# First query and key products together while x arrives, first value products around the row norm, and program order on three engines until then

## The chip, the cores and the metric

The kernel runs on one core of a Trainium2 chip. The metric is device time in microseconds (us) for one launch. Five engines work side by side: TensorE (PE, with its weight loads as PEld), VectorE (DVE), ScalarE (ACT), GpSimd (POOL) and SyncE (SP), which issues all transfers between memory and the chip. Each engine takes its instructions in one fixed order and waits at an instruction until what it needs is there.

## The reference

One inference step of an encoder layer over 576 new rows plus 16 learned rows (592 in all, `T`), width 2048. The part that matters here is the beginning:

```
h = x * rsqrt(mean(x*x) + eps) * g                # RMSNorm of every row
z = h @ w_in                                      # 2048 -> 3904 columns
q, k, v of 8 differential heads = slices of z     # 128 columns each
... two softmaxes per head with a shared relative-position bias, their difference times v
... a second group of latent-attention heads, output projection, SwiGLU feed-forward, final norm
```

`q`, `k` and `v` of head 0 are the first three 128-column slices that the kernel makes. The norm's factor of a row is a scalar, so it can be applied after the product.

## The kernel before, in words

Every float32 product is split: each operand becomes a high and a low part (`xh`, `xl`; `wh`, `wl`), and three products are added up in PSUM (`mm3`, three matmuls for each of two halves of 296 rows; called a triple below). ScalarE casts the high part, VectorE subtracts to get the low part. So every chunk of x and every block of weights passes ScalarE and then VectorE before TensorE can use it.

The stage in question opens the program. x arrives in four column groups of 512 columns (`load_x`), each in six row tiles (`tok`) with seven transfers. For each of 16 chunks of 128 columns, `transpose_x` lets TensorE transpose the six tiles into PSUM (`pxt`, one two-bank tile, for even chunks; `pxa` and `pxb`, single banks, for odd ones), ScalarE and VectorE split the result with the gain into `xh`, `xl`, VectorE copies the plain transpose to `xt`, and SyncE stores `xt` to `xspill` for the residual addition much later. `xt` has three buffers (`Z_BUFS`), so the copy of a chunk waits until the store of three chunks before has landed. After chunk 3 of each group the squares of the group's six tiles are summed on ScalarE (`ssp`).

Between the transposes stand the triples of head 0's queries alone (`first = project(ps0, ...)`), one per chunk. Then come the norm (`ss`, `rc`, `rb`; six small matmuls into `prb` spread the factor over all partitions), the bias table (`ptr`, `trs`, `trow`, and `tsk`, eight broadcast stores of 328 KB), and then `projections()`: keys and values of head 0, then queries, keys and values of heads 1 to 7. `natural` transposes keys and values back for the outputs, and `diff_attend` does the attention of a head; its first matmuls write `sp`. Weights come in blocks of 1024 x 128 (`wr`, 512 KB), two per projection.

TensorE's order is the order in which the code calls it. For the projections and the attention that order is set by `Streams`, a planner in the kernel: it keeps a clock `now` that each matmul moves on, banks (`sp`, `tp`, `po`) with times at which they come free, and streams with ranks; the projections are the filler of lowest rank. VectorE's, ScalarE's and SyncE's orders are chosen when the program is built, by a scheduler that takes what it thinks ready first. GpSimd has a few memsets in this stage.

Of the kernel before, what the change touches and what calls it, by code (L numbers as in the profile page):

```python
# [111 lines left out]
        self.tc.keep_in_program_order(self.pe.transpose(out, in_, identity))  # L112


@with_exitstack
def encoder_step(
    ctx: ExitStack,
# [16 lines left out]
    S.preload_act_table_set("natural_log_exp_and_others")  # L134

    def load(dst, src):
        nc.sync.dma_start(dst, src)

    def store(dst, src):
        nc.sync.dma_start(dst, src)  # L140

    def const(name, shape, src):
        t = cp.tile(shape, F32, name=name)
# [19 lines left out]
    def rsqrt(r, v):  # L163

        S.activation(r, v, AF.Ln)
        S.activation(r, r, AF.Exp, scale=-0.5)
        V.tensor_tensor(v, v, r, op=ALU.mult)
        V.scalar_tensor_tensor(v, v, -0.5, r, op0=ALU.mult, op1=ALU.mult)
        V.scalar_tensor_tensor(r, v, 1.5, r, op0=ALU.add, op1=ALU.mult)
# [144 lines left out]
    with ExitStack() as ph:  # L314
# [7 lines left out]
        def pjt():  # L322
            return pj.tile([P, 2, 512], F32, name="ps", tag="ps")
# [4 lines left out]
        def tbank(name="tp"):  # L328
            return pst.tile([P, 512], F32, name=name, tag="tp")
# [11 lines left out]


        tok = [(0, OWN), (OWN, P), (208, 88), (TH, P), (424, P), (552, 40)]
        ps0 = pjt()
        with tc.tile_pool(name="xn", bufs=1) as xn:
            ssp = az.tile([P, 6, 4], F32, name="ssp")
            V.memset(ssp, 1.0)
            junk = xn.tile([P, 512], F32, name="junk")
            xt_in = {}

            def load_x(cg):
                cs = slice(cg * 512, (cg + 1) * 512)
                for j, (o, n) in enumerate(tok):
                    t = xn.tile([P, 512], F32, name="xn", tag=f"xn{j}", bufs=2)
                    if j == 0:
                        load(t[0:NS, :], x_sample[:, cs])
                        load(t[NS:OWN, :], meta[:, cs])
                    else:
                        load(t[0:n, :], x_prompt[o - OWN:o - OWN + n, cs])
                    xt_in[cg, j] = t  # L360

            def transpose_x(kc):
                cg, k = kc // 4, kc % 4
                if kc % 2 == 0:
                    sp = sbig("pxt")
                    banks = [sp[:, 0, 0:TH], sp[:, 1, 0:TH]]
                else:
                    banks = [tbank("pxa")[:, 0:TH], pso.tile([P, 512], F32, name="pxb", tag="po")[:, 0:TH]]
                for j, (o, n) in enumerate(tok):
                    b = o // TH  # L370
                    PE.transpose(banks[b][:, o - b * TH:o - b * TH + n],
                                 xt_in[cg, j][0:n, k * P:(k + 1) * P], ident[0:n, 0:n])
                xt = ztile("xt")
                g = gA[:, kc:kc + 1]
                if kc % 2 == 0:
                    split_scaled(hv(xh[kc]), hv(xl[kc]), ev(sp), g)
                    V.tensor_copy(hv(xt), ev(sp))
                else:
                    for b in range(2):
                        c = slice(b * TH, (b + 1) * TH)  # L380
                        split_scaled(xh[kc][:, c], xl[kc][:, c], banks[b], g)
                        V.tensor_copy(xt[:, c], banks[b])
                for o, n, c in KEPT:
                    store(xspill[kc, :, c:c + n], xt[:, o:o + n])
                if k == 3:
                    for j, (o, n) in enumerate(tok):
                        S.activation(junk[0:n], xt_in[cg, j][0:n], AF.Square, accum_out=ssp[0:n, j, cg:cg + 1])
                    if cg + 2 < 4:
                        load_x(cg + 2)

            load_x(0)
            gains = xn.tile([P, P], F32, name="gains")
            V.memset(gains, 0.0)
            rows = 0
            for g in (g_attn, g_ffn, g_fin, g_q, g_kv, g_sub):
                n = g.shape[0] // P
                load(gains[rows:rows + n, :], g.rearrange("(c p) -> c p", p=P))
                rows += n
# [6 lines left out]
            first = project(ps0, w_in[:, 0:P], xs1)  # L405
# [18 lines left out]
        ss = az.tile([P, 6], F32, name="ss")  # L424
        rc = az.tile([P, 6], F32, name="rc")
        V.reduce_sum(ss, ssp, axis=AX.X)
        V.tensor_scalar(ss, ss, 1.0 / D, EPS, op0=ALU.mult, op1=ALU.add)
        rsqrt(rc, ss)
        pb = sbig("prb")
        for j, (o, n) in enumerate(tok):  # L430
            b = o // TH
            PE.matmul(pb[:, b, o - b * TH:o - b * TH + n], rc[0:n, j:j + 1].to_broadcast([n, P]),
                      ident[0:n, 0:n], start=True, stop=True)
        V.tensor_copy(hv(rb), ev(pb))

        with tc.tile_pool(name="xc", bufs=1, side="right") as xc:

            oh = xc.tile([32, NREL], F32, name="oh")
            load(oh, c_onehot)
            rbt = xc.tile([32, H], F32, name="rbt")  # L440
            load(rbt, rel_bias)
            ptr = sbig("ptr")
            trs = xc.tile([H, NREL], F32, name="trs")
            for i, (a, b) in enumerate(((0, 512), (512, NREL))):
                PE.matmul(ptr[0:H, i, 0:b - a], rbt, oh[:, a:b], start=True, stop=True)
                V.tensor_copy(trs[:, a:b], ptr[0:H, i, 0:b - a])
            store(trow, trs)
            for h in range(H):
                nc.sync.dma_start(tsk[h], trow[h:h + 1, :].to_broadcast([P, NREL]))

            lamt = xc.tile([P, 4, DH], F32, name="lamt")
            load(lamt, lam_p.rearrange("a b -> (a b)").unsqueeze(0).to_broadcast([P, 4 * DH]).rearrange(
                "p (a b) -> p a b", a=4))
            lprod = xc.tile([P, 2, DH], F32, name="lprod")
            lsum = xc.tile([P, 2], F32, name="lsum")
            V.tensor_tensor(lprod, lamt[:, 0:4:2, :], lamt[:, 1:4:2, :], op=ALU.mult)
            V.reduce_sum(lsum, lprod, axis=AX.X)
            S.activation(lsum, lsum, AF.Exp)
            V.memset(lamv[:, 0:1], 1.0)
            V.tensor_tensor(lamv[:, 1:2], lsum[:, 0:1], lsum[:, 1:2], op=ALU.subtract)  # L460
            V.tensor_scalar(lamv[:, 1:2], lamv[:, 1:2], LAM_INIT, None, op0=ALU.add)
            V.tensor_scalar(g08, g08, 1.0 - LAM_INIT, None, op0=ALU.mult)

        zl_cm = tc.tile_pool(name="zl", bufs=1, side="right")
        zl = zl_cm.__enter__()
# [110 lines left out]

        def projections():
            for h in range(H):
                ps = ps0 if h == 0 else pjt()
# [10 lines left out]
                ps = pjt()  # L590
                yield from project(ps, w_in[:, OFF_K + h * P:OFF_K + (h + 1) * P], xs1)
                if h >= 1:
                    yield [nat[2 * h - 1], nat[2 * h - 2]]
                z = ztile()
# [3 lines left out]
                split(kh[:, 0:T], kl[:, 0:T], z)  # L598
                nat[2 * h] = st.spawn(0, keys(h, z, kh, kl))

                ps = pjt()
                yield from project(ps, w_in[:, OFF_V + h * P:OFF_V + (h + 1) * P], xs1)
                if h >= 2:
                    yield [att[h - 2]]
                z = ztile()
                V.tensor_tensor(hv(z), ev(ps), hv(rb), op=ALU.mult)
                vh = ap.tile([P, 6, P], F32R, name="vh", bufs=2)
                vl = ap.tile([P, 6, P], F32R, name="vl", bufs=2)
                nat[2 * h + 1] = st.spawn(0, values(h, z, vh, vl))
# [10 lines left out]
        for name in ("sp", "tp", "po"):  # L620
            st.bank(name, 1)
        st.spawn(9, projections())
        st.run()

# [816 lines left out]
```

## Time and profile before

| what | value |
|---|---|
| median of 3 runs | 2577.13 us (2576.43 to 2582.49) |
| the profiled execution's own time | 2573.65 us |
| its span, first to last instruction | 2571.8 us |
| mean granted TensorE clock | 0.985 |
| TensorE busy | 2458.2 us, 96% |
| VectorE busy | 1839.6 us, 72% |
| ScalarE busy | 1056.4 us, 41% |
| transfers | 307.74 MB, mean 120 GB/s |

The profiled execution is 3.5 us below the median of the runs. Times inside the trace are counted from the span's start. A timeline row reads: start, duration, engine, line, operation, output<-inputs, shape, count, and in brackets the idle time before it with what ended it. A waits row reads: who waited for whom, us in total, times, longest.

### The profile page before, as it was taken

The numbers are of one execution on the slowest core, as the hardware profiler recorded it, in microseconds if no ns is written. First come the engines' busy times: TensorE is split into PE (matmuls) and PEld (weight loads), VectorE is DVE, ScalarE is ACT, GpSimd is POOL, SyncE is SP. The second block draws the span as 40 slices with busy tenths as digits, with TensorE's granted clock in tenths as the row PEclk, the third lists the DMA queues.
The fourth block names the chain that finished last, engine by engine and source line by source line (L and its number), as shares of the span: only waits on it lengthen the run. The fifth ranks groups of instructions, "written<-read, shape, count | busy, mean of one in ns | idle before, by whom it ended". The sixth has DMA issues, their size and how long they took to land. (4 is left out here: it accounts for less than half of the span.)

```text
span 2571.8 us, 44874 instructions
## 1 busy us (share of the span) xinstructions
PE 2458.2 (96%) x17847; PEld 2394.0 (93%) x17847; DVE 1839.6 (72%) x2955; ACT 1056.4 (41%) x1879; POOL 770.6 (30%) x614
## 2 busy tenths in 40 slices
PE   6999999989999999999999999999999899999997
PEld 5999999988999888999999999999999799999997
DVE  5455555556555568877777777777778999999975
ACT  5234333334443444333333333333334444444445
POOL 0000000000000164554645546454553322222236
PEclk9999999999999899999999999999999899999999
DMA  6433222334332453333333333333344643452334
GB/s 205 132 89 87 79 81 82 85 99 131 93 94 76 154 155 108 122 131 117 122 102 118 131 117 129 108 110 127 117 135 141 212 151 95 147 163 83 109 100 148
DMA packets 330564, 307.74 MB, mean 120 GB/s; under 512 B 24707, under 2 KB 298506, under 8 KB 330354
## 3 DMA queue, kind: packets, MB, share of 16 engines
q1 hardware_dynamic: 330354, 304.87, 37.5%
q8 instruction: 140, 2.29, 0.4%
q14 instruction: 70, 0.57, 0.1%
HBM read 250.82 MB, written 56.68 MB: 120 GB/s over the span
## 5 line engine op out<-in xcount | busy, mean ns | idle before, releaser
L1051 PE MATMUL m<-bh,wh 128*128 128x288 f32 x3584 | 969.1, 296 | 12.5 <-ACT wh L156 10.4
L1051 PE MATMUL m<-bl,wh 128*128 128x288 f32 x3584 | 967.7, 295 | 0.0
L1051 PEld LDWEIGHTS m<-bh,wh 128*128 128x128 f32 x3584 | 674.2, 188 | 15.1 <-ACT wh L156 12.7
L1051 PEld LDWEIGHTS m<-bl,wh 128*128 128x128 f32 x3584 | 677.9, 189 | 0.1
L1055 PE MATMUL m<-bh,wl 128*128 128x288 f32 x3584 | 588.7, 299 | 29.5 <-DVE wl L153 27.0
L1020 POOL TENSOR_TENSOR ws<-raw 128x512 f32<-128x512 f32 x256 | 364.7, 1433 | 753.4 <-DVE wl L153 517.7
L1055 PEld LDWEIGHTS m<-bh,wl 128*128 128x128 f32 x3584 | 511.8, 189 | 47.0 <-DVE wl L153 46.0
L156 ACT ACTIVATE wh<-ws 128x512 fp32r<-128x512 f32 (+1 forms) x340 | 288.6, 849 | 471.6 <-PE m L1051 341.4
L153 DVE TENSOR_TENSOR wl<-ws,wh 128x512 fp32r<-128x512 f32 (+1 forms) x340 | 380.5, 1124 | 57.4 <-ACT wh L156 52.8
L153 DVE TENSOR_TENSOR wl<-raw,wh 128x512 fp32r<-128x512 f32 x416 | 401.6, 986 | 13.8 <-ACT wh L156 13.2
L156 ACT ACTIVATE wh<-raw 128x512 fp32r<-128x512 f32 x416 | 248.0, 626 | 334.5 <-PE m L1051 303.5
L108 PE MATMUL ps<-xh,wh 128*128 128x296 f32 x992 | 229.5, 313 | 6.5 <-ACT wh L156 6.5
L108 PE MATMUL ps<-xl,wh 128*128 128x296 f32 x992 | 219.8, 303 | 0.0
L108 PE MATMUL ps<-xh,wl 128*128 128x296 f32 x992 | 219.2, 303 | 0.0
L108 PEld LDWEIGHTS ps<-xh,wh 128*128 128x128 f32 x992 | 163.8, 193 | 10.4 <-ACT wh L156 6.7
L108 PEld LDWEIGHTS ps<-xl,wh 128*128 128x128 f32 x992 | 164.6, 192 | 0.4 <-DVE xl L161 0.2
L108 PEld LDWEIGHTS ps<-xh,wl 128*128 128x128 f32 x992 | 164.2, 192 | 0.3 <-DVE wl L153 0.3
L1020 DVE TENSOR_TENSOR ws<-ws,raw 128x512 f32<-128x512 f32 x128 | 96.1, 755 | 90.4 <-POOL ws L1020 85.4
L153 DVE TENSOR_TENSOR wl<-wr,wh 128x1024 fp32r<-128x1024 f32 (+1 forms) x110 | 117.8, 1071 | 44.4 <-ACT wh L156 42.5
L1272 DVE TENSOR_TENSOR y<-y,m 128x288 f32<-128x288 f32 x280 | 125.6, 449 | 19.3 <-PE m L1055 18.1
L156 ACT ACTIVATE wh<-wr 128x1024 fp32r<-128x1024 f32 (+1 forms) x110 | 101.8, 930 | 79.9 <-PE ps L108 71.4
L518 POOL MEMSET bias<- 64x64 f32 x8 | 1.4, 180 | 413.7 <-DMA bias<-tsk 184.8
(361 smaller groups left out, 3420.0 us busy)
## 6 DMA issues: line engine op xcount, KB each, us to landing
raw<-in_ffn_w_gate SPq DMA_DIRECT2D x44, 1024.0 KB, 7.2
raw<-in_ffn_w_up SPq DMA_DIRECT2D x44, 1024.0 KB, 6.0
raw<-in_ffn_w_down SPq DMA_DIRECT2D x40, 1024.0 KB, 5.4
wr<-in_w_in SPq DMA_DIRECT2D x60, 512.0 KB, 3.7
actspill<-c SPq DMA_DIRECT2D x44, 288.0 KB, 2.2
sumspill<-c SPq DMA_DIRECT2D x20, 576.0 KB, 3.0
bl<-sumspill SPq DMA_DIRECT2D x80, 144.0 KB, 3.1
bl<-actspill SPq DMA_DIRECT2D x68, 144.0 KB, 3.9
```

What stands on the lines that cost most here:

```text
L108: self.tc.keep_in_program_order(self.pe.matmul(out, lhsT, rhs, start=start, stop=stop))
L153: V.tensor_tensor(lo, src, f32(hi), op=ALU.subtract)
L156: S.activation(hi, src, AF.Copy)
L518: G.memset(bias[0:64, 464:528], -BIG)
L1020: engine.tensor_tensor(w[:, k:k + m, :], pick(xs), pick(ys), op=op)
L1051: PE.matmul(banks[p], wh[:, k, :], x, start=first and new and k == 0 and x is hi, stop=False, skip_group_check=not new)
L1055: PE.matmul(banks[p], wl[:, k, :], hi, start=False, stop=last and k == n - 1, skip_group_check=not new)
L1272: V.tensor_tensor(c, c, banks[p], op=ALU.add)
```

## The change

- A small class `Engine` wraps VectorE, ScalarE and SyncE. While its flag is set, the instructions keep the order of the code; the flag is set from the first load of the stage to the end of the bias table's broadcasts.
- The loads of the gains, the one-hot table `oh` and `rel_bias` come ahead of x. The weights of head 0's first half of queries and of keys come after the first x group, those of the second half after the second, and the third and fourth x group follow at once (four buffers a tile in place of two). All of this stands ahead of the first `xspill` store.
- The bias table's two matmuls come ahead of the first transpose.
- Each chunk now has two triples, queries (`psq`) and keys (`psk`). The squares are spread over the chunks of a group.
- The values of head 0 (`psv`, in the bank pair of `sp`) follow: eight triples, the norm's six small matmuls, eight triples. The first value weights are loaded and cast at chunk 10.
- `projections()` starts with all three of head 0 done; the planner's bank `sp` starts taken and comes free when `psv` has been read.

The core of the diff:

```diff
+class Engine:
...
+        def call(*args, **kwargs):
+            ins = issue(*args, **kwargs)
+            return self.tc.keep_in_program_order(ins) if self.ordered else ins
...
-    V, S, G = nc.vector, nc.scalar, nc.gpsimd
+    V, S, Q, G = Engine(tc, nc.vector), Engine(tc, nc.scalar), Engine(tc, nc.sync), nc.gpsimd
...
+        psq, psk, psv = pjt(), pjt(), None
+        for e in (V, S, Q):
+            e.ordered = True
...
-                    t = xn.tile([P, 512], F32, name="xn", tag=f"xn{j}", bufs=2)
+                    t = xn.tile([P, 512], F32, name="xn", tag=f"xn{j}", bufs=4)
...
             load_x(0)
+            raws = [raw_weights(wp, 0, 0), raw_weights(xn, 0, OFF_K)]
             load_x(1)
+            raws += [raw_weights(wp, 8 * P, 0), raw_weights(xn, 8 * P, OFF_K)]
+            load_x(2)
+            load_x(3)
...
             transpose_x(0)
+            ws = [split_raw(wp, raws[0])]
+            transpose_x(1)
+            ws.append(split_raw(xn, raws[1]))
             for kc in range(KC):
-                if kc + 1 < KC:
-                    transpose_x(kc + 1)
-                next(first)
+                if kc:
+                    if kc + 1 < KC:
+                        transpose_x(kc + 1)
+                    squares(kc // 4, ((), (0,), (1, 2), (3, 4, 5))[kc % 4])
+                if kc in (4, 6):
+                    ws.append(split_raw((wp, xn)[kc // 2 - 2], raws[kc // 2]))
+                elif kc == 8:
+                    store(trow, trs)
+                elif kc == 10:
+                    raws.append(raw_weights(wp, 0, OFF_V))
+                    ws.append(split_raw(wp, raws[4]))
+                elif kc == 12:
+                    raws.append(raw_weights(wp, 8 * P, OFF_V))
+                for i, ps in enumerate((psq, psk)):
+                    wh, wl = ws[kc // 8 * 2 + i]
+                    mm3([ps[:, 0, 0:TH], ps[:, 1, 0:TH]], wh[:, kc % 8, :], wl[:, kc % 8, :],
+                        halves(xh[kc]), halves(xl[kc]), kc == 0, kc == KC - 1)
+            psv = sbig("psv")
...
+            rsqrt(rc, ss)
+            first_values(0)
+            ws.append(split_raw(wp, raws[5]))
...
+            first_values(1)
...
+            for h in range(H):
+                Q.dma_start(tsk[h], trow[h:h + 1, :].to_broadcast([P, NREL]))
+        for e in (V, S, Q):
+            e.ordered = False
```

Three places show how the instructions move. First SyncE's queue, where the first stores of `xt` (chunks 0 and 1) stand. Before, they follow the second x group and one block of weights:

```order
L137 DMA xn<-in_x_prompt 40x512
L137 DMA wr<-in_w_in 128x8x128
L140 DMA xspill<-xt 128x64
L140 DMA xspill<-xt 128x512
L140 DMA xspill<-xt 128x64
L140 DMA xspill<-xt 128x512
L137 DMA wr<-in_w_in 128x8x128
```

Now, from the fourth x group on:

```order
L125 DMA xn<-in_x_sample 64x512
L125 DMA xn<-in_meta_tokens 16x512
L125 DMA xn<-in_x_prompt 128x512
L125 DMA xn<-in_x_prompt 88x512
L125 DMA xn<-in_x_prompt 128x512 x2
L125 DMA xn<-in_x_prompt 40x512
L125 DMA lamt<-in_diff_lambda 128x256
L125 DMA xspill<-xt 128x64
L125 DMA xspill<-xt 128x512
```

The first store has moved from behind two x groups and one weight block to behind all four x groups, four weight blocks and `lamt`.

Second, ScalarE around chunks 11 and 12 (`xh_103` and `xh_104`; `wh<-wr` is the cast of a weight block, `junk` a square). Before:

```order
L160 ACTIVATE xh_103<-pxa,gT 128x296
L160 ACTIVATE xh_103<-pxb,gT 128x296
L387 ACTIVATE junk,ssp<-xn 80x512
L387 ACTIVATE junk,ssp<-xn 128x512
L387 ACTIVATE junk,ssp<-xn 88x512
L387 ACTIVATE junk,ssp<-xn 128x512 x2
L387 ACTIVATE junk,ssp<-xn 40x512
L160 ACTIVATE xh_104<-pxt,gT 128x592
```

Now:

```order
L125 ACTIVATE xh_103<-pxa,gT 128x296
L125 ACTIVATE xh_103<-pxb,gT 128x296
L125 ACTIVATE junk,ssp<-xn 128x512
L125 ACTIVATE junk,ssp<-xn 88x512
L125 ACTIVATE wh<-wr 128x1024
L125 ACTIVATE xh_104<-pxt,gT 128x592
```

The cast of the first value weights now stands between the two chunks; the load of those weights is issued on SyncE directly behind the two stores of chunk 11.

Third, TensorE at chunks 0 and 1 (`xh_92`, `xh_93`). Before:

```order
L108 MATMUL ps<-xh_92,wh 128x296 x2
L108 MATMUL ps<-xl_108,wh 128x296 x2
L108 MATMUL ps<-xh_92,wl 128x296 x2
L112 MATMUL pxt<-ident,xn 128x80
L112 MATMUL pxt<-ident,xn 128x128
```

Now:

```order
L108 MATMUL ps<-xh_92,wh 128x296 x2
L108 MATMUL ps<-xl_108,wh 128x296 x2
L108 MATMUL ps<-xh_92,wl 128x296 x2
L108 MATMUL ps<-xh_92,wh 128x296 x2
L108 MATMUL ps<-xl_108,wh 128x296 x2
L108 MATMUL ps<-xh_92,wl 128x296 x2
L112 MATMUL pxt<-ident,xn 128x80
L112 MATMUL pxt<-ident,xn 128x128
```

A second triple, that of the keys, stands between the transposes of two chunks. Further down, 62 triples stand ahead of the first score matmul (`sp`) of head 0 before and 71 now: 48 of head 0 in both, then 14 and 23 of head 1's queries and keys, because the `natural` transposes of head 0's keys no longer stand among its value triples. At the first score of heads 1, 2 and 3 the counts are 125, 181 and 236 before and 132, 187 and 238 now; by the end of head 3 both stand at 256.

More of the change, by code (lines that the diff above doesn't have):

```diff
@@ L112, in transpose, with __init__, __getattr__ @@
         self.tc.keep_in_program_order(self.pe.transpose(out, in_, identity))
+class Engine:
+    def __init__(self, tc, engine):
+        self.tc, self.engine, self.ordered = tc, engine, False
+    def __getattr__(self, name):
+        issue = getattr(self.engine, name)
+        def call(*args, **kwargs):
+            ins = issue(*args, **kwargs)
+            return self.tc.keep_in_program_order(ins) if self.ordered else ins
+        return call
 @with_exitstack
@@ L343, in encoder_step @@
         tok = [(0, OWN), (OWN, P), (208, 88), (TH, P), (424, P), (552, 40)]
-        ps0 = pjt()
-        with tc.tile_pool(name="xn", bufs=1) as xn:
+        psq, psk, psv = pjt(), pjt(), None
+        for e in (V, S, Q):
+            e.ordered = True
+        with tc.tile_pool(name="xn", bufs=1) as xn, tc.tile_pool(name="xc", bufs=1, side="right") as xc:
+            gains = xn.tile([P, P], F32, name="gains")
+            V.memset(gains, 0.0)
+            rows = 0
+            for g in (g_attn, g_ffn, g_fin, g_q, g_kv, g_sub):
+                n = g.shape[0] // P
+                load(gains[rows:rows + n, :], g.rearrange("(c p) -> c p", p=P))
+                rows += n
+            oh = xc.tile([32, NREL], F32, name="oh")
+            load(oh, c_onehot)
+            rbt = xc.tile([32, H], F32, name="rbt")
+            load(rbt, rel_bias)
             ssp = az.tile([P, 6, 4], F32, name="ssp")
@@ L384, in transpose_x, with squares, raw_weights, split_raw @@
                     store(xspill[kc, :, c:c + n], xt[:, o:o + n])
[L385 to L389, printed above, removed]
-            load_x(0)
[L392 to L398, printed above, removed]
-            load_x(1)
+            def squares(cg, js):
+                for j in js:
+                    n = tok[j][1]
+                    S.activation(junk[0:n], xt_in[cg, j][0:n], AF.Square, accum_out=ssp[0:n, j, cg:cg + 1])
+            def raw_weights(pool, r0, c0):
+                wr = pool.tile([P, 8, P], F32, name="wr", tag="wr", bufs=WR_BUFS)
+                load(wr, w_in[r0:r0 + 8 * P, c0:c0 + P].rearrange("(k p) c -> p k c", p=P))
+                return wr
+            def split_raw(pool, wr):
+                wh = pool.tile([P, 8, P], F32R, name="wh", tag="wh", bufs=WH_BUFS)
+                wl = pool.tile([P, 8, P], F32R, name="wl", tag="wl", bufs=WH_BUFS)
+                split(wh, wl, wr)
+                return wh, wl
+            load_x(0)
+            raws = [raw_weights(wp, 0, 0), raw_weights(xn, 0, OFF_K)]
+            load_x(1)
+            raws += [raw_weights(wp, 8 * P, 0), raw_weights(xn, 8 * P, OFF_K)]
+            load_x(2)
+            load_x(3)
+            lamt = xc.tile([P, 4, DH], F32, name="lamt")
+            load(lamt, lam_p.rearrange("a b -> (a b)").unsqueeze(0).to_broadcast([P, 4 * DH]).rearrange(
+                "p (a b) -> p a b", a=4))
             pg = tbank("pg")
@@ L404, in encoder_step @@
             gA, gF, gE, gq, gkv, g08 = (gT[:, a:b] for a, b in ((0, 16), (16, 32), (32, 48), (48, 52), (52, 54), (54, 55)))
-            first = project(ps0, w_in[:, 0:P], xs1)
+            trs = xc.tile([H, NREL], F32, name="trs")
+            ptr = sbig("ptr")
+            for i, (a, b) in enumerate(((0, 512), (512, NREL))):
+                PE.matmul(ptr[0:H, i, 0:b - a], rbt, oh[:, a:b], start=True, stop=True)
+                V.tensor_copy(trs[:, a:b], ptr[0:H, i, 0:b - a])
             transpose_x(0)
+            ws = [split_raw(wp, raws[0])]
@@ new lines, in encoder_step, with first_values @@
+            psv = sbig("psv")
+            def first_values(hf):
+                wh, wl = ws[4 + hf]
+                for k in range(8):
+                    kc = 8 * hf + k
+                    mm3([psv[:, 0, 0:TH], psv[:, 1, 0:TH]], wh[:, k, :], wl[:, k, :],
+                        halves(xh[kc]), halves(xl[kc]), kc == 0, kc == KC - 1)
+            ss = az.tile([P, 6], F32, name="ss")
+            rc = az.tile([P, 6], F32, name="rc")
+            V.reduce_sum(ss, ssp, axis=AX.X)
+            V.tensor_scalar(ss, ss, 1.0 / D, EPS, op0=ALU.mult, op1=ALU.add)
@@ new lines, in encoder_step @@
+            rsqrt(rc, ss)
+            first_values(0)
+            ws.append(split_raw(wp, raws[5]))
+            pb = [tbank("prb"), pso.tile([P, 512], F32, name="prb", tag="po")]
+            for j, (o, n) in enumerate(tok):
+                b = o // TH
+                PE.matmul(pb[b][:, o - b * TH:o - b * TH + n], rc[0:n, j:j + 1].to_broadcast([n, P]),
+                          ident[0:n, 0:n], start=True, stop=True)
+            for b in range(2):
+                V.tensor_copy(rb[:, b * TH:(b + 1) * TH], pb[b][:, 0:TH])
@@ new lines, in encoder_step @@
+            first_values(1)
+            lprod = xc.tile([P, 2, DH], F32, name="lprod")
+            lsum = xc.tile([P, 2], F32, name="lsum")
+            V.tensor_tensor(lprod, lamt[:, 0:4:2, :], lamt[:, 1:4:2, :], op=ALU.mult)
+            V.reduce_sum(lsum, lprod, axis=AX.X)
+            S.activation(lsum, lsum, AF.Exp)
+            V.memset(lamv[:, 0:1], 1.0)
+            V.tensor_tensor(lamv[:, 1:2], lsum[:, 0:1], lsum[:, 1:2], op=ALU.subtract)
+            V.tensor_scalar(lamv[:, 1:2], lamv[:, 1:2], LAM_INIT, None, op0=ALU.add)
@@ L422, in encoder_step @@
             G.memset(pt_b[b][:, 0:NS], 0.0)
[L424 to L462, printed above, removed]
         zl_cm = tc.tile_pool(name="zl", bufs=1, side="right")
@@ L599, in projections @@
                 nat[2 * h] = st.spawn(0, keys(h, z, kh, kl))
-                ps = pjt()
-                yield from project(ps, w_in[:, OFF_V + h * P:OFF_V + (h + 1) * P], xs1)
+                ps = pjt() if h else psv
+                if h:
+                    yield from project(ps, w_in[:, OFF_V + h * P:OFF_V + (h + 1) * P], xs1)
                 if h >= 2:
@@ L606, in projections @@
                 V.tensor_tensor(hv(z), ev(ps), hv(rb), op=ALU.mult)
+                if h == 0:
+                    st.give("sp", 1.5)
                 vh = ap.tile([P, 6, P], F32R, name="vh", bufs=2)
@@ L618, in projections @@
                 V.tensor_tensor(hv(zs[i]), ev(ps), hv(rb), op=ALU.mult)
-        for name in ("sp", "tp", "po"):
-            st.bank(name, 1)
+        for name, n in (("sp", 0), ("tp", 1), ("po", 1)):
+            st.bank(name, n)
         st.spawn(9, projections())
```

12 lines of the change are left out of this document (7 added, 5 removed).

## The prediction

> **What bounds the kernel now.** I read the page first, then TensorE's waits in the first 100 us, its timeline there, and the transfers and the clock by windows. The page:
>
> ```profile
> span 2571.8 us, 44874 instructions
> PE 2458.2 (96%) x17847; PEld 2394.0 (93%) x17847; DVE 1839.6 (72%) x2955; ACT 1056.4 (41%) x1879; POOL 770.6 (30%) x614
> ```
>
> TensorE is busy 96% of the span, so time is gained where it idles or runs at half clock. The change touches the first 92 us. TensorE's waits there:
>
> ```profile
> PE pg L112 <- DMA gains<-in_diff_subln_g: 9.8, 1, 9.8
> PE ps L108 <- ACT wh L156: 6.5, 1, 6.5
> PE pxa L112 <- DVE xt L382: 5.1, 2, 2.8
> PE ptr L108 <- DVE rb L434: 0.9, 1, 0.9
> PE ptr L108 <- DVE trs L446: 0.8, 1, 0.8
> PE prb L108 <- DVE rc L169: 0.6, 1, 0.6
> ```
>
> That is 23.7 us: a late start, a wait for the first weights, two waits for copies of chunks, and the bias table beside the norm. The timeline prices the work between (two pieces of it, and the VectorE row that ends the stretch):
>
> ```profile
> 19.26 0.86 PE L108 MATMUL ps<-xh,wh 128*128 128x296 f32 x2 [6.50 <-ACT wh L156]
> 22.49 0.86 PE L108 MATMUL ps<-xh,wh 128*128 128x296 f32 x2
> 24.13 0.69 PE L112 MATMUL pxa<-ident,xn 80*128 80x80 f32 x3
> 25.44 0.82 PE L108 MATMUL ps<-xh,wh 128*128 128x296 f32 x2
> 26.64 0.83 PE L112 MATMUL pxt<-ident,xn 80*128 80x80 f32 x6
> 28.32 0.43 PE L112 MATMUL pxa<-ident,xn 80*128 80x80 f32 x3
> 58.35 1.69 PE L108 MATMUL prb<-ident,rc 80*128 80x80 f32 x12 [0.64 <-DVE rc L169]
> 70.40 0.44 PE L108 MATMUL ps<-xh,wh 128*128 128x296 f32 x2
> 71.22 0.43 PE L108 MATMUL ps<-xh,wh 128*128 128x296 f32 x2
> 91.77 0.78 DVE L606 TENSOR_TENSOR z<-ps,rb 128x592 f32<-128x592 f32 x1 [2.32 <-PE ps L108]
> ```
>
> Early, before TensorE is warm, a triple takes 22.49 to 24.13 = 1.64 us and a chunk's transposes 24.13 to 25.44 = 1.31. Later a chunk's transposes with one triple take 26.64 to 28.32 = 1.68, and a triple alone 70.40 to 71.22 = 0.82; so transposes with two triples will take 1.68 + 0.82 = 2.50. Head 0's values are done at 91.77.
>
> ```profile
> 10.00:20.00 10.00, 3.50 (x16) 2.61 (x16) 4.26 (x9) 7.25 (x18) 0.00 (x0) 1.00 0.91 279
> 16.00:20.00 4.00, 0.74 (x3) 0.74 (x4) 0.76 (x1) 2.50 (x5) 0.00 (x0) 1.00 1.11 357
> 28.00:30.00 2.00, 2.00 (x16) 1.78 (x15) 1.70 (x3) 1.18 (x3) 0.00 (x0) 1.00 0.78 217
> 28.00:36.00 8.00, 7.51 (x52) 6.20 (x50) 7.13 (x13) 6.19 (x17) 0.00 (x0) 1.00 0.91 280
> 40.00:42.00 2.00, 2.00 (x10) 1.59 (x9) 0.87 (x4) 0.71 (x1) 0.00 (x0) 0.50 0.61 174
> 50.00:52.00 2.00, 2.00 (x9) 1.58 (x8) 2.00 (x4) 1.01 (x2) 0.00 (x0) 0.50 0.61 179
> ```
>
> These window rows end in granted clock, transfer share and GB/s. Long stretches with a full queue move 280 GB/s, short ones 217 to 357. The clock falls to 0.50 after each of the two waits for chunk copies (2.2 and 2.8 us). A drop costs about 1.7 us: half the speed for some 3.4 us (40 to 42 at 0.50, and part of the windows beside it).
>
> **The change part by part.** The transfers first, because they now set the pace.
>
> ```profile
> 0.73 0.39 SPq L137 DMA_DIRECT2D ident<-c_ident  x1
> 1.18 0.59 SPq L137 DMA_DIRECT2D xn<-in_x_sample  x1
> xn<-in_x_prompt SPq DMA_DIRECT2D x4, 176.0 KB
> xn<-in_x_sample SPq DMA_DIRECT2D x4, 128.0 KB
> xn<-in_meta_tokens SPq DMA_DIRECT2D x4, 32.0 KB, 2.5
> wr<-in_w_in SPq DMA_DIRECT2D x10, 512.0 KB, 5.4
> DMA to landing us min/median/max: 3.7/5.4/6.0
> 66.77 5.17 SPq L449 DMA_DIRECT2D tsk<-trow  x8
> ```
>
> (The landing row is that of the weight blocks `wr`.) Nine issues now stand ahead of x at some 0.45 us each (0.73 to 1.18), so x's first issue moves from 1.18 to about 4.8 and its data flow from about 7 on. An x group is 1184 KB (128 + 32 + 3 x 256 + 176 + 80; the three of 256 KB and the one of 80 KB are the other row tiles) = 1.21 MB, a weight block 0.52 MB. At 280 GB/s the first group and the first block, 1.74 MB, land at 7 + 6.2 = 13.2; with the cast of about 1.1 us the first triple starts near 14.5 instead of 19.26. The early start of `pg` and `ptr` on the small loads costs nothing: it fills the wait for x and takes the waits of 0.9 and 0.8 us out of the norm's place.
>
> Chunks 0 to 2 are then done by about 26: one and a half of them at the early speed of 2 x 1.64 + 1.31 = 4.59, the rest at 2.50, with the keys' first block landing 1.9 us behind the queries'. Chunk 3 stops. Its copy to `xt` needs the buffer of chunk 0, whose store now stands behind all of x, four weight blocks and `lamt`: 4 x 1.21 + 4 x 0.52 + 0.13 = 7.08 MB, 25.3 us at 280 GB/s, so 32.3; the store of 0.29 MB takes it to 33.3, and copy and split of the two halves on VectorE (program order holds the split behind the copy) to about 34.2. This wait is in no row of before; between 217 and 357 GB/s it ends at 41.9 and 28.5. I take 34.2, since 280 is what both long windows show. TensorE idles some 8 us, and the clock drops once: 1.7.
>
> [...]
>
> From 34.2 on thirteen chunks remain. With transposes of chunk 4 already done and none after the last, they take 13 x 2.50 - 2 x 0.86 = 30.8. At chunk 12 ScalarE stands at the cast of the value weights, whose load SyncE issues only after the stores of chunk 11: from the start of chunk 10's turn some 3 us until chunk 11 is copied, 1.2 for three issues, 3.7 to 6.0 for the landing, 1.06 for the cast and 0.76 for chunk 12's own cast, so 9.7 to 12.0. TensorE wants chunk 12 after 2 x 2.50 + 0.86 = 5.9. The stall is 3.8 to 6.1; I take 4.5, since few transfers are queued then, and one more drop of 1.7. Other work of ScalarE and VectorE is behind the same cast, but it is all of later chunks. The values take 16 x 0.82 + 1.69 (`prb`) = 14.8; the norm's chain hides behind the first eight triples. The squares, spread over the chunks, hide too:
>
> ```profile
> L387 ACT ACTIVATE junk<-xn x24: 617/630/634, 4.4 to 48.0; 128x512 f32<-128x512 f32 x12, 80x512 f32<-80x512 f32 x4, 88x512 f32<-88x512 f32 x4, 40x512 f32<-40x512 f32 x4
> ```
>
> (ns, least, median, most.) With the read-out about 0.8 us each, one and a half a chunk and a cast of 0.8 make 2.0 of ScalarE's time in a turn of 2.50; without that room they would lengthen the turn.
>
> Sum: 34.2 + 1.7 + 30.8 + 4.5 + 1.7 + 14.8 = 87.7, against 91.77: 4.1 us earlier. The eight `tsk` transfers (2.7 MB, 9.6 us at 280) now stand ahead of head 1's second weight block, which is wanted 6.6 us after 87.7; issued from about 73 on they are through at about 84, so that is covered by some 8 us.
>
> What follows keeps only part of that:
>
> ```profile
> 103.59 0.23 PE L108 MATMUL sp<-kh,q00h 128*128 128x144 f32 x1
> 167.74 0.23 PE L108 MATMUL sp<-kh,q10h 128*128 128x144 f32 x1
> 396.98 0.23 PE L108 MATMUL sp<-kh,q10h 128*128 128x144 f32 x1
> 452.35 0.23 PE L108 MATMUL sp<-kh,q00h 128*128 128x144 f32 x1
> PE sp L108 <- DVE nm L533: 5.4, 5, 1.9
> 307.89 0.27 PE L108 MATMUL sp<-kh,q11h 128*64 128x128 f32 x1 [1.94 <-DVE nm L533]
> 309.00:313.00 4.00, 4.00 (x20) 4.00 (x19) 2.93 (x8) 0.69 (x3) 0.00 (x0) 0.57 0.49 138
> ```
>
> (First scores of heads 0, 1, 5 and 6; TensorE's waits for VectorE's score reduction in 92 to 600, the first of them, and the window behind it.) Nine more triples stand ahead of the first score (71 against 62), so it moves from 103.59 to 87.7 + 9 x 0.82 + 11.8 = 106.9: later by 3.3, though the stage is done earlier. By the end of head 3 both orders have done 256 triples and the same attention, so as long as TensorE does not idle more, the 4.1 us stand. But heads 0 to 3 have nine triples less to fill with. Before, the waits for score reductions came to 5.4 us in five, the first at 307.89, with a clock of 0.57 behind it. The extra lies between none and one more such place at full size (1.9 + 1.7 = 3.6). I take the mean wait, 1.1, and half a drop, 0.9: 2.0. Feed-forward and all behind it keep their order.
>
> Net: 4.1 - 2.0 = about 2 us faster, 2571.6 for an execution like the profiled one (2573.65) and, since that lies 3.5 below the median of the runs, 2575.1 as a median.
>
> **The rivals.** *Fast transfers (chance 0.28).* The loads no longer wait for compute, so the queue is always full, and 357 GB/s as in 16 to 20 holds all along. Then the store of chunk 0 lands at 7 + 7.37 / 0.357 = 27.6, chunk 3 goes on at 28.5, and without a long idle the drop goes too: 5.7 + 1.7 = 7.4 more, in all 9.4 faster, 2567.7. For it: the row of 357. Against: it lasted 4 us, and 10 to 20 as a whole, with a queue about as full, gave 279. [...]
>
> *The attention's own chain sets the heads' spacing (chance 0.17), slower.* From 396.98 to 452.35 a head takes 55.4 us, from 103.59 to 167.74 it took 64.1. If the early heads are held by VectorE and ScalarE and not by the filler, none catches up: the first score's delay of 3.3 stays to the end, with one more wait and drop of 3.6: 6.9 slower, 2584.0. It decides where head 0 still takes over 63 us with nine triples (7.4 us) less filler. Against: the first wait for a score reduction comes only at 307.89, so until then filler covered the chain.
>
> *Slow transfers (chance 0.10).* At 217 GB/s as in 28 to 30 chunk 3 goes on at 7 + 7.37 / 0.217 + 0.9 = 41.9, 7.7 later: 5.7 slower, 2582.8. That it does not do what it says (keys not filling) has no chance left to speak of: the triples stand there.
>
> **How the numbers follow.** The forecast, 2575, has 0.45, and its own range is 2570 to 2580. The upper end of all, 2587, is the attention rival with the weights' landing at its longest and a little of the slow transfers; the lower, 2564, is the fast rival with no extra waits and the value weights landing in 3.7 (9.4 + 2.0 + 1.5 = 12.9 faster). Within 0.3%, about what a measurement of this kernel can tell from no change, is 2569.4 to 2584.9. Most of the fast rival lies below (0.25, with 0.03 of the forecast); about half of the attention rival and of the slow one lies above, with some of both together: 0.20. The rest is 0.52.
>
> **What would show it.** Right: first triple at 14 to 15; one TensorE wait for a VectorE row of chunk 3 (`xl` behind `xt`) of 5 to 9 us ending near 34; one of 4 to 5 for ScalarE's `xh` at chunk 12, near 60; both with clock 0.50 behind; head 0's values done near 88; first score near 107; one or two more waits for `nm` before 300. Wrong: transfers over 330 GB/s between 8 and 30 with no wait at chunk 3; value weights there in time; or a spacing of over 63 us from head 0 to head 1.

## The result, and the profile after

The change makes no difference that the runs can tell: 2578.48 us (median of 12 runs, 2575.82 to 2583.66) against 2578.44 for the kernel before on the same chip (12 runs, 2575.46 to 2582.49). The ratio is 1.0001, its 95% interval 0.9993 to 1.0009, or -1.8 to +2.3 us. The forecast was 2575.0, in the range 2564 to 2587, with "within 0.3%" as the likeliest outcome.

The page of the kernel after, its two lines that answer to those of before:

```profile
span 2577.7 us, 44857 instructions
PE 2460.2 (95%) x17847; PEld 2394.5 (93%) x17847; DVE 1838.0 (71%) x2956; ACT 1055.7 (41%) x1879; POOL 766.3 (30%) x614
```

This execution took 2579.44 us, 1.0 above its median; the one profiled before was 4.8 below the median of its later runs. So the 5.9 us between the two spans are no measure of the change. The runs are, and the traces tell where time sits.

TensorE's waits in the first 100 us (who waited for whom, us in total, times, longest):

```profile
PE ps L108 <- DVE xl L125: 7.9, 2, 7.4
PE pg L112 <- DMA gains<-in_diff_subln_g: 4.6, 1, 4.6
PE ps L108 <- ACT xh L125: 3.5, 1, 3.5
PE ps L108 <- ACT wh L125: 2.2, 2, 1.4
PE pxt L112 <- DMA xn<-in_x_prompt: 2.0, 3, 1.2
```

The waits of 9.8 and 6.5 at the start have shrunk to 4.6 and 2.2, and the two for chunk copies (5.1) are gone. In their place stand one of 7.4 and one of 3.5. TensorE's timeline at these two, and at the first triple, the norm's matmuls and the first two value matmuls:

```profile
16.63 0.86 PE L108 MATMUL ps<-xh,wh 128*128 128x296 f32 x2 [1.37 <-ACT wh L125]
37.53 0.61 PE L108 MATMUL ps<-xl,wh 128*128 128x296 f32 x1 [7.41 <-DVE xl L125]
65.81 0.86 PE L108 MATMUL ps<-xh,wh 128*128 128x296 f32 x2 [3.46 <-ACT xh L125]
67.18 0.86 PE L108 MATMUL ps<-xl,wh 128*128 128x296 f32 x2 [0.50 <-DVE xl L125]
76.93 0.43 PE L108 MATMUL psv<-xh,wh 128*128 128x296 f32 x2
83.49 1.62 PE L108 MATMUL prb<-ident,rc 80*128 80x80 f32 x12
```

The timelines of the three engines behind them name the causes: VectorE's copy of chunk 3 waits for a store of `xt`, and ScalarE's cast of the value weights for their load. Then head 0's values are read out:

```profile
36.58 0.47 DVE L125 COPY xt<-pxa 128x296 f32<-128x296 f32 x1 [8.88 <-DMA xspill<-xt]
64.06 1.06 ACT L125 ACTIVATE wh<-wr 128x1024 fp32r<-128x1024 f32 x1 [4.80 <-DMA wr<-in_w_in]
65.03 0.74 ACT L125 ACTIVATE xh<-pxt,gT 128x592 fp32r<-128x592 f32 x1
91.90 0.78 DVE L125 TENSOR_TENSOR z<-psv,rb 128x592 f32<-128x592 f32 x1
```

SyncE's timeline has the store and the load behind these waits, the first store of `xt` issued at 31.92, the value weights at 59.77:

```profile
4.36 0.59 SPq L125 DMA_DIRECT2D xn<-in_x_sample  x1
9.04 4.33 SPq L125 DMA_DIRECT2D xn<-in_x_sample  x1
26.43 0.48 SPq L125 DMA_DIRECT2D xn<-in_x_sample  x1
31.92 8.98 SPq L125 DMA_DIRECT2D xspill<-xt  x10
59.77 0.38 SPq L125 DMA_DIRECT2D wr<-in_w_in  x1
```

Windows of the same trace (the last three columns are granted clock, transfer share and GB/s):

```profile
8.00:33.00 25.00, 17.20 (x71) 12.83 (x71) 8.15 (x13) 10.11 (x21) 0.00 (x0) 1.00 0.94 257
37.50:43.50 6.00, 5.97 (x24) 5.54 (x25) 4.08 (x8) 1.96 (x3) 0.00 (x0) 0.50 0.33 107
65.80:71.00 5.20, 4.68 (x18) 3.97 (x18) 3.70 (x7) 2.81 (x8) 0.00 (x0) 0.51 0.21 72
```

Behind the two waits TensorE works for 6.0 and 4.7 us at half clock (its busy time in the last two rows). Head 0's values are read out at 91.90, and were at 91.77 before: what the earlier start saved, the two waits and their clock took back.

The first scores of heads 0, 1, 5 and 6, and TensorE's waits between 92 and 600 that concern the heads:

```profile
113.26 0.23 PE L108 MATMUL sp<-kh,q00h 128*128 128x144 f32 x1
176.12 0.31 PE L108 MATMUL sp<-kh,q10h 128*128 128x144 f32 x1
400.51 0.23 PE L108 MATMUL sp<-kh,q10h 128*128 128x144 f32 x1
455.95 0.23 PE L108 MATMUL sp<-kh,q00h 128*128 128x144 f32 x1
PE sp L108 <- DVE nm L125: 7.1, 8, 1.6
PE pnb L112 <- DVE na L125: 1.3, 1, 1.3
PE tp L112 <- DVE pol L125: 0.6, 1, 0.6
```

The gap to before is 9.7 us at head 0, 8.4 at head 1, and 3.5 and 3.6 at heads 5 and 6. Two thirds of the first score's delay are caught up on the way.

### The profile page after: what moved, and what is told of

Its sections match the earlier page's. It is cut to its first block, busy times and chain, and to the rows that moved or that the text cites. A ratio compares the mean times of both kernels' runs of the same rounds, so it can differ in the third digit from the quotient of the medians.

```text
span 2577.7 us, 44857 instructions
## 1 busy us (share of the span) xinstructions
PE 2460.2 (95%) x17847; PEld 2394.5 (93%) x17847; DVE 1838.0 (71%) x2956; ACT 1055.7 (41%) x1879; POOL 766.3 (30%) x614
## 5 line engine op out<-in xcount | busy, mean ns | idle before, releaser
L1116 PE MATMUL m<-bh,wh 128*128 128x288 f32 x3584 | 970.1, 296 | 11.9 <-ACT wh L125 9.9
L108 PE MATMUL ps<-xh,wh 128*128 128x296 f32 x960 | 222.9, 314 | 5.6 <-ACT xh L125 3.5
L108 PE MATMUL ps<-xl,wh 128*128 128x296 f32 x960 | 212.9, 303 | 7.9 <-DVE xl L125 7.9
L108 PE MATMUL ps<-xh,wl 128*128 128x296 f32 x960 | 212.6, 303 | 0.0
L108 PEld LDWEIGHTS ps<-xl,wh 128*128 128x128 f32 x960 | 159.2, 192 | 8.5 <-DVE xl L125 8.5
L108 PEld LDWEIGHTS ps<-xh,wl 128*128 128x128 f32 x960 | 159.0, 192 | 0.5 <-DVE wl L125 0.5
L125 DVE TENSOR_TENSOR y<-y,m 128x288 f32<-128x288 f32 x312 | 139.8, 448 | 26.3 <-PE m L1120 18.1
L125 DVE TENSOR_TENSOR c<-s,m 128x288 f32<-128x288 f32 x176 | 75.1, 446 | 94.4 <-DMA sumspill<-c 91.7
```

Source lines behind the costliest of these rows:

```text
L108: self.tc.keep_in_program_order(self.pe.matmul(out, lhsT, rhs, start=start, stop=stop))
L125: ins = issue(*args, **kwargs)
L1116: PE.matmul(banks[p], wh[:, k, :], x, start=first and new and k == 0 and x is hi, stop=False, skip_group_check=not new)
```

## The experiments

Theory W: the time is TensorE's work and its waits; what the beginning wins or loses reaches the end, less the few more waits among the early heads. Rival H: the heads' own pace, or the time of the first score, sets the end. Rival R: the transfers' rate sets the beginning, whatever stands in the way.

All nine in one table. "Values" is the start of TensorE's last value matmul of head 0 in the trace; the difference is that of the medians to the kernel before in the same series of runs.

| kernel | median, us (runs) | before, us | difference | ratio, 95% | values |
|---|---|---|---|---|---|
| before | | | | | 91.4 |
| change | 2578.48 (12) | 2578.44 | 0.0 | 0.9993 to 1.0009 | 91.6 |
| e1, seven copies of `xt` | 2570.57 (9) | 2577.69 | -7.1 | 0.9960 to 0.9983 | 82.0 |
| e2, value weights earlier | 2574.11 (12) | 2577.69 | -3.6 | 0.9973 to 0.9994 | 84.8 |
| e3, both | 2566.37 (6) | 2577.69 | -11.3 | 0.9939 to 0.9968 | 74.9 |
| e4, no program order | 2577.24 (12) | 2577.69 | -0.5 | 0.9984 to 1.0006 | 87.7 |
| e5, values in the stream | 2578.02 (11) | 2576.79 | +1.2 | 0.9996 to 1.0015 | 93.0 |
| e6, e1 and e2 and e5 | 2564.73 (5) | 2576.79 | -12.1 | 0.9933 to 0.9960 | 74.6 |
| e7, x behind the stores | 2568.99 (6) | 2576.79 | -7.8 | 0.9956 to 0.9979 | 81.2 |
| e8, before, seven copies | 2573.24 (12) | 2578.80 | -5.6 | 0.9969 to 0.9991 | 86.8 |
| e9, e6 with x first | 2565.01 (6) | 2578.80 | -13.8 | 0.9937 to 0.9961 | 76.3 |

**e1: the wait at chunk 3.** More copies of `xt`, so that none waits for a store:

```diff
-                xt = ztile("xt")
+                xt = xn.tile([P, T], F32, name="xt", tag="xt", bufs=7)
```

> The changed kernel with seven buffers for the copies xt in place of three shared ones; nothing else. Theory W (TensorE work: what is won ahead of the attention reaches the end, less new waits): the wait of 7.4 us at chunk 3 and the half clock behind it (6 us at 0.50, 3 us lost) go; head 0's values done near 81 instead of 91.6, first score near 103, the whole about 9 us below the changed kernel, near 2569. Rival H (VectorE and ScalarE set the heads' pace): values as early, but the gain is given back in heads 0 to 3, end within 2 us of 2578. Rival R (transfer rate): chunk 4, 8 or 12 waits for x instead, values not before 88.

Measured: 7.1 below before. TensorE's waits in the first 100 us now begin with:

```profile
PE pg L112 <- DMA gains<-in_diff_subln_g: 4.6, 1, 4.6
PE ps L108 <- ACT xh L125: 4.3, 1, 4.3
PE pxt L112 <- DMA xn<-in_x_prompt: 1.6, 2, 1.0
PE ps L108 <- ACT wh L125: 1.4, 2, 1.0
```

The wait of 7.4 is gone and no transfer has taken its place; what remains for x is 1.6. R does not hold, and H would have left the end where it was.

**e2: the wait at chunk 12.** The first value weights are loaded at chunk 5; their cast stays at chunk 10:

```diff
+                elif kc == 5:
+                    raws.append(raw_weights(wp, 0, OFF_V))
...
                 elif kc == 10:
-                    raws.append(raw_weights(wp, 0, OFF_V))
                     ws.append(split_raw(wp, raws[4]))
```

> The changed kernel with the load of the first value weights issued at chunk 5 instead of chunk 10; its cast stays at chunk 10. Theory W: the 3.5 us wait at chunk 12, 0.5 behind it and 2.5 of half clock go; values done near 85, the whole 5 to 6 below the changed kernel, near 2573. Rival H: values as early, end within 2 us of 2578. If the cast itself and not the load held ScalarE, the wait at chunk 12 stays above 2 us.

Measured: 3.6 below before, somewhat less than expected, with the interval holding both. Of the two waits only that at chunk 3 is left in the trace:

```profile
PE ps L108 <- DVE xl L125: 8.2, 1, 8.2
PE pg L112 <- DMA gains<-in_diff_subln_g: 4.6, 1, 4.6
```

**e3: both.**

> Both edits together: seven copies and the value weights loaded at chunk 5. Theory W: values near 75, the whole about 14 below the changed kernel, near 2564. Rival H: end within 2 us of 2578, first head's spacing longer by what the start has won.

Measured: 11.3 below before; the two alone add up to 10.7. TensorE's waits in the first 100 us, and that for score reductions between 92 and 600:

```profile
PE pg L112 <- DMA gains<-in_diff_subln_g: 4.7, 1, 4.7
PE pxt L112 <- DMA xn<-in_x_prompt: 3.1, 3, 2.6
PE ps L108 <- ACT wh L125: 1.1, 1, 1.1
PE sp L108 <- DVE nm L125: 7.1, 8, 1.6
```

The stage ends 16.7 us earlier than with the change. The granted clock is 1.00 from 28 to 44 us and from 60 to 75, where it is 0.68 and 0.77 with the change. The waits for `nm` are what they were. Not all of the 16.7 us reaches the end, which is 11.3 earlier.

**e4: the program order.** The change with `e.ordered = False`, so that the scheduler chooses VectorE's, ScalarE's and SyncE's orders again:

```diff
         for e in (V, S, Q):
-            e.ordered = True
+            e.ordered = False
```

> The changed kernel with the flag never set: VectorE, ScalarE and SyncE in the order that the scheduler picks at build time; TensorE's order is unchanged. If program order itself makes the two waits (stores behind all of x, value weights behind the stores of chunk 11), they shrink or go: values near 84 to 87 and the whole 4 to 6 below the changed kernel, near 2573. If the order of the code is what lets the keys fill the waits, waits for casts behind squares come back as before (two of 2 to 3 us) and the whole is 0 to 5 above it.

Measured: 0.5 below before, with an interval from -4.1 to +1.5; the expected 4 to 6 below the change are not shown. The trace shows why the gain is small: one of the two waits went and the other grew. The wait at chunk 12 is gone, with the value weights issued at 45.70 in place of 59.77. At chunk 3 TensorE waits longer than with the change, now in front of a transpose:

```profile
PE pxa L112 <- DVE xt L125: 9.8, 1, 9.8
PE pg L112 <- DMA gains<-in_diff_subln_g: 4.8, 1, 4.8
```

The stores still stand behind all four x groups: SyncE issues the first at 31.52, against 31.92. The two that free the buffer are issued by 31.9; with the 4.2 us that the slowest such store took to land in the trace of the change (first 70 us) they are through by an estimated 36.1, but VectorE copies only at 40.72. The scheduler has put work of the norm in front of the copy, and that waits for ScalarE's squares:

```profile
31.52 11.65 SPq L125 DMA_DIRECT2D xspill<-xt  x10
45.70 1.13 SPq L125 DMA_DIRECT2D wr<-in_w_in  x2
39.46 0.18 DVE L125 TENSOR_REDUCE ss<-ssp 128x6 f32<-128x24 f32 x1 [4.05 <-ACT junk L125]
40.72 0.46 DVE L125 COPY xt<-pxa 128x296 f32<-128x296 f32 x1
```

So both expectations showed in part. Program order makes the wait at chunk 12; at chunk 3 it keeps VectorE's copy ahead of the norm's work. Since all three engines were set free together, the run does not say which engine's order made the wait at chunk 12; e2 shows that an earlier load is enough to remove it.

**e5: the first score's time.** The second half of head 0's values becomes part of the planner's stream, so that the `natural` transposes of the keys stand among its triples again, as before the change (`first_values` becomes a generator for this, in lines left out here):

```diff
...
-            first_values(1)
...
                 if h:
                     yield from project(ps, w_in[:, OFF_V + h * P:OFF_V + (h + 1) * P], xs1)
+                else:
+                    yield from first_values(1)
```

> The second eight value triples of head 0 (first_values(1)) move from the fixed beginning into the planner's stream, so that the natural transposes of head 0's keys may stand among them, as they did before the change. Theory W (the end is the beginning's TensorE work plus waits, so the first score's time does not matter by itself): the first score comes some 8 to 10 us earlier than with the change (near 104 in place of 113), the heads 4 to 7 keep a gap of at most 1 to 3 us to the change, by the waits for nm that go (7.1 us in 8 with the change), and the end is 0 to 3 us below 2578.5. Rival H (the time of the first score sets the heads and the end): the end follows, 7 to 9 below.

Measured: +1.2 to before, with an interval from -1.0 to +3.9, where the change had 0.0. The first score comes at 106.9 in place of 113.3, and the end does not follow. H is refuted in this form. TensorE's waits for score reductions fell, and that for `na` is gone:

```profile
PE sp L108 <- DVE nm L125: 5.7, 7, 0.9
```

**e6: all three edits.**

> The three edits together: seven copies of xt, value weights loaded at chunk 5, and the second half of the first values in the planner's stream. W: no wait at chunk 3 or 12, first score near 87 to 90 (96.8 with the first two alone), values done near 75 as there, and the end as with the first two edits or up to 3 below: 2563.5 to 2566.4. H: first score's 8 to 10 us come off the end: near 2558.

Measured: 12.1 below before. The first score is at 89.3, 7.5 earlier than in e3, and the end is 0.8 further below before, which the intervals cannot tell from nothing. W again.

**e7: the store's place in the queue.** Three buffers of `xt` as in the change, but the third and fourth x group are issued at chunks 2 and 5, behind the first stores:

```diff
-            load_x(2)
-            load_x(3)
...
+                if kc in (2, 5):
+                    load_x(2 + kc // 4)
```

> The third and fourth x groups are issued at chunks 2 and 5, behind the first stores of xt, with three buffers of xt as in the change. If the store's place in SyncE's queue makes the wait at chunk 3: the wait of 7.4 is gone, no clock drop behind it, the value wait at chunk 12 stays (3 to 5), and the end is 5 to 8 us below 2578.5, near the 7.9 that seven copies gave. If three buffers of xt are too few wherever the store stands, or the transfers' total rate sets the pace: a wait for xt or for x of 4 to 8 us appears between chunks 3 and 12 all the same, and the end is within 2 of 2578.5.

Measured: 7.8 below before. VectorE's wait for stores of `xt` in the first 60 us, 8.9 in one piece with the change, is now:

```profile
DVE xt L125 <- DMA xspill<-xt: 2.5, 3, 1.5
```

So three buffers were enough. The store's place behind 7.08 MB of loads made the wait, as the prediction had it: SyncE issues the first store at 21.42 here and at 31.92 with the change.

**e8: the same cure for the old order.** The edit of e1 in the kernel before the change.

> The kernel before the change with one edit: seven copies of xt in place of three. Its two waits for chunk copies (5.1 us together, clock 0.50 behind each) should go. W: 5.1 and two drops, 8.5 at most, 5 to 8.5 below before; then the old order has the same cure as the new one (7.9 for the change with seven copies), and the change gains nothing even without the wait at chunk 3. Rival O (the new order is worth something once its own wait is gone, since before's chunks are bound by the arrival of x and by ScalarE's squares instead): the waits turn into waits for x or for xh, and the end is within 3 of before.

Measured: 5.6 below before, in the range of W. In part the other rival showed too; TensorE's wait for x in the first 100 us, not there before, is

```profile
PE pxt L112 <- DMA xn<-in_x_prompt: 2.5, 4, 1.6
```

Behind it TensorE still slows down once: two matmuls of 296 columns that took 0.43 to 0.44 us at 40.13 and 40.41 take 0.69 at 44.79 and 45.28, and 0.43 again at 48.05. So of the two drops that W let go, one stayed.

With one edit each, old and new order lie 5.6 and 7.1 below before, and their intervals overlap. With both of its own waits gone the new order lies 11.3 below (e3), and ends the stage 11.9 us ahead of e8. So at the end the new order is worth about 6 us (11.3 against 5.6, with intervals that just do not overlap), and the change as made hides it.

**e9: x ahead of the small loads.** e6, with `load_x(0)` moved ahead of the gains, `oh` and `rel_bias`.

> The three edits together, and the first x group issued ahead of the gains, oh and rel_bias (nine issues, 3.2 us of SyncE's time, between 1.18 and 4.36). W: the first triple starts 2 to 3 earlier than the change's 16.6 and the end is 2 to 3 below the kernel with the three edits (near 2562). Rival T (the transfers' rate sets the first triple, since gains and x share the same engines): first triple within 0.7 of 16.6 and the end within 1 of that kernel.

Measured: 13.8 below before, not distinguishable from e6. The first triple came at 17.63, not sooner than in the other traces of the new order (15.5 to 17.5), and for neither theory's reason. TensorE's timeline:

```profile
9.82 0.45 PE L112 MATMUL pg<-ident,gains 128*128 128x128 f32 x1 [9.82 <-DMA gains<-in_mla_q_norm_g]
10.74 1.86 PE L108 MATMUL ptr<-oh,rbt 32*8 32x512 f32 x2 [0.48 <-DMA rbt<-in_rel_bias]
14.40 1.44 PE L112 MATMUL pxt<-ident,xn 80*128 80x80 f32 x6 [0.39 <-DVE trs L125]
17.63 0.61 PE L108 MATMUL ps<-xh,wh 128*128 128x296 f32 x1 [0.42 <-ACT wh L125]
```

The gains are issued behind x, from 4.69 to 7.80 in place of 1.18 to 3.24, and `pg` and `ptr` stand in TensorE's order ahead of x's transposes: the wait moved from x to the small loads. Whether x first helps with `ptr` further back was not tried.

e3, e6 and e9 are the fastest, about 0.5% below before. The intervals do not rank them; e3 is the smallest, two short edits.

## Why the prediction was right, and which terms were off

**The outcome** "within 0.3%" held, and the two waits that the sum put into the new order are both there, at their places and for their reasons (the copy of chunk 3 behind a store, chunk 12 behind the value weights' cast). e1, e7 and e2 took away one cause each, and each wait went with its cause. The sum still came out 3.5 us too fast as a median. Of these, 1.3 are its base, since the three runs of before known then had a median of 2577.13 and the twelve have 2578.44; the rest is that 2.1 faster was forecast and 0.0 measured. The terms, one by one:

- *First triple near 14.5*: 16.63. The first group and block arrive slower than 280 GB/s would bring them: ScalarE's cast of the first block starts at 15.52, not at 13.2. This term did not reach the end, since chunk 3 waits for the store anyway.
- *Chunk 3 goes on at 34.2*: 37.53. This is the step that was mis-sized. The full queue moved 257 GB/s from 8 to 33, not 280: 7.08 MB from 7 on then take 27.5, the store 1.1, copy and split 0.9, and 36.5 comes out, so the rate is 2.3 of the 3.3, and the last 1.0 stays open. That the store comes through only behind the loads ahead of it was an assumption of this sum, which no run showed at the time; in its place stand the 31.92 of its issue and the 36.58 of VectorE's copy with the change, and e7, where waits for these stores came to 2.5 with the longest 1.5. The "slow transfers" rival at 217 had 41.9; the truth lay between, nearer to the forecast. The "fast transfers" rival, 357 GB/s, did not happen: from 8 to 33 the traces of the new order show 239 to 263.
- *Each drop 1.7*: about 3.0 and 2.3. TensorE worked 6.0 and 4.7 us at half clock behind the two waits (the window rows), where 3.4 was assumed. Together 1.9 more.
- *Stall at chunk 12, 4.5*: 3.46 and 0.50, so 4.0.
- *Values 14.8*: from 76.93 to 91.70 (the next projection's first matmul), 14.8.
- *Values done at 87.7*: 91.90. The 4.2 are 3.3 of the restart, 1.9 of the clock and 0.2 up to the read-out, less 0.5 at the stall and 0.7 in the turns between. The gain of 4.1 from the stage became none.
- *First score at 106.9*: 113.26. Of the 6.4, 4.2 are the later values; the rest is the `natural` work of the keys, which now stands behind the values, with a wait of 1.3 for `na`.
- *Extra waits 2.0*: in the trace of after 3.6 (7.1 + 1.3 + 0.6 against 5.4), while the clock fell to 0.50 twice in 300 to 450 us (for 3.4 us from 313.2 and from 422.5) where it fell three times before (from 309.4, 364.0 and 418.6). The table gives a better measure. In the nine kernels with the new order, what the values gained against before minus what the end gained is between -0.4 and 5.2 us, 2.4 in the mean; for the change itself it is -0.2. The traces put it at the projections' end: there the six kernels in which all first values stand ahead of the planner have lost 0.7 to 4.8 us of what their values gained, 2.8 in the mean, and the three with e5's edit between -2.4 and 0.4. The size of the term was about right as a mean, and no single pair of runs shows it.

Corrected by 4.2 later and 1.6 more of waits in that trace, the sum gives 3.7 slower than before, and the projections' end is indeed 3.6 later in the trace (572.13 against 568.53, the last triple). The runs say 0.0, between -1.8 and +2.3. So part of this 3.7 belongs to the two executions that happened to be profiled; which part stays open.

**The attention rival** is refuted in its mechanism. It was to decide where head 0 takes over 63 us: it takes 62.9 (113.26 to 176.12), just under the mark. But the mark was misread: the nine triples of filler are not all missing in head 0. By the counts ahead of the prediction 61 triples stand between the first scores of heads 0 and 1 now, and 63 before; two at 0.82 take 64.1 to 62.5, and 62.9 is 0.4 above that. So VectorE and ScalarE hardly hold this head. The later heads agree: 6.2 of the 9.7 us of delay are caught up by head 5, and e5 moved the first score by 6.4 without the end following.

## What to carry to other kernels

Loading ahead moves later stores back in the same queue (the first of `xt` was issued at 31.92 with the change and at 21.42 in e7): before all loads are put in front, look for the buffer whose release hangs on the first store behind them, and either add copies of it or let the store go between the loads. An engine held to the code's order needs each load issued several steps ahead of the instruction that uses it, or everything behind that instruction waits too (here ScalarE waited 4.80 us and TensorE 3.46 behind it; e2, with the load at chunk 5, has no such wait of TensorE); left to the scheduler, it may get other waiting work put in front (e4, where VectorE waited 4.05 us for squares). When a large reordering moves nothing, cure its own new waits before judging the order, and give the old order the same cure as a control.

## What the runs showed of the hardware

**The clock came back late after the long waits.** Before the change, waits of 2.2 and 2.8 us were each followed by one stretch of 3.4 us at half clock (from 39.7 and from 50.0). With the change, the clock was at half from 33.3 to 43.6 around the wait of 7.41 (10.2 us, 6.0 of them after work had resumed) and from 64.1 to 70.9 around that of 3.46 (6.8 us): three and two times the 3.4 of before. Before has a third such stretch in the stage, which the prediction does not list: the clock is 0.50 from 63.6 to 67.0, behind three waits of 0.6 to 0.9 us around the norm and the bias table.

**The window rows do not show the slow start.** They give a clock of 1.00 from 8 us on, but two matmuls of the first triple with the change take 0.86 us at 16.63, as long as at 65.81 under half clock. Only at about 27 us do such rows fall to 0.43 us. The first record of the clock stands at 26.1 us in the trace of before and at 26.5 in that of the change.

**The store came through behind the loads.** With the change, the first store of `xt` stood behind seven megabytes of loads; it was issued at 31.92, and the copy that needs its buffer went on at 36.58, after a wait of 8.88. With the third and fourth x group behind it (e7) it was issued at 21.42, and VectorE's waits for stores of `xt` came to 2.5 us, the longest 1.5.

**An issue can take several us.** An issue of `xn<-in_x_sample` on SyncE took 0.59 us at 4.36 and 4.33 us at 9.04, behind two weight blocks. No run tested why.

**One execution says little about a few us.** From the projections' last triple to the end no edit changes anything, yet that stretch took 2003.3 us in the trace of before and 2005.6 in that of the change, and the profiled executions lay between 6.4 below and 4.8 above the medians of their kernels.
